# Dilated attention in a hybrid encoder layer: where the softmax's division stands

## The chip, the cores and the metric

The kernel runs on one core of a Trainium2 chip. The core has a matrix engine (PE, with its weight loads shown as PEld), a vector engine (DVE), a scalar engine (ACT), a general engine (POOL), a queue engine that issues most transfers (SP) and 16 DMA engines. The metric is the device time of one execution, in microseconds. Each engine runs its instructions in order; they wait for each other by semaphores.

## The reference

One layer of an encoder over 512 tokens of width 2048, all in float32: a retention branch and a dilated attention branch side by side, gated and merged, then a layer of 16,384 single-neuron experts of which each token takes 16 for each of 8 heads. The change is in the attention branch alone. Cut to that:

```python
ATT_SEGMENTS = ((128, 1), (512, 4), (2048, 16))      # (window, dilation), 8 heads of 128 each
s = einsum('nbihd,nbjhd->nbhij', qb, kb) * d ** -0.5 # masked outside the window
m = max(s, -1); p = exp(s - m); l = sum(p, -1)
o = einsum('nbhij,nbjhd->nbihd', p / l, vb);  lse = m + log(l)
...
w = softmax(stack(lses), axis=0)                     # over the three (window, dilation) groups
o = einsum('gbsh,gbshd->bshd', w, stack(outs))
```

Since the groups are merged by their denominators, a head's three groups are one softmax: one maximum, one sum over the three groups' exponentials, and one weighted sum of their values. The kernel computes it so.

## The kernel before, in words

The 512 tokens are four tiles of 128 (tile r holds the tokens r, r+4, ...). The front of the kernel, `mixers(part, with_kv)`, runs twice: part 0 for one token tile (T = 1), with the keys and values of all tiles, and part 1 for the other three (T = 3). In each part two blocks `hb` of four attention heads follow the projections that they need, so there are four stretches of four heads: two of part 0, two of part 1. Weights come in chunks of 512 KB (`wraw`), which ACT splits into a high half (`whi`, L130) and DVE into a low half (`wlo`, L131); each chunk feeds matmuls `gB` (L146 to L148), three per tile and 128 rows.

One head (`att_head`, L412 to L482) goes so. PE makes scores into PSUM banks (`sc`, L429 for group 0, 128x512, L437 for groups 1 and 2, 128x128 per tile). DVE adds the mask, takes the maximum and writes them to `P0` and `P1` (L431, L439), and makes the negative maximum `nb`. ACT takes the exponentials in place and sums each row (L449, nine in part 1, three in part 0). DVE adds the three sums to `lt` and inverts it (L452 to L454). Then DVE multiplies the exponentials by `lt` (L461, L468), PE transposes them to `pT` (L462, L471), ACT copies these to SBUF (`pT1s` L464, `pT0s` L473), PE multiplies them with the values (L476, L478) and sums over keys into the bank `oT`, 128 columns per token tile. As written before, the values are the stationary operand and the result comes out with the head's dimensions on the partitions and the tokens along the row. ACT copies it to `aT` (L480), and SP stores it to DRAM (`attD`, L482), where the merge (L553) reads it later. All banks named here come from `psB`, a pool of four.

In part 1 the experts of part 0 are worked in between: POOL gathers rows of the expert tables (L753, 1 MB each) and DVE multiplies and sums them (`gr`, L762). `tick(inv, 2)` behind the reciprocal places two such products behind it in DVE's order, and weight chunks place more by `tick(low, 0.85)`.

Which instruction follows which on an engine isn't the order of the code. A scheduler sets it when the kernel is built, from dependencies, free buffers and its own estimates; weight matmuls of the next projection are put between the instructions of the heads.

Of the kernel before, what the change touches and what calls it, by code (L numbers as in the profile page):

```python
# [10 lines left out]
F32 = mybir.dt.float32  # L11
# [4 lines left out]
AF = mybir.ActivationFunctionType  # L16
ALU = mybir.AluOpType
AX = mybir.AxisListType

P = 128  # L20
# [7 lines left out]
HD = 128  # L28
# [36 lines left out]
def hybrid_layer(ctx, tc, I, out, dbg=None):  # L65
    nc = tc.nc
# [33 lines left out]
    ident = const.tile([P, P], F32, name="ident")  # L100
# [3 lines left out]
    def bank(name, pool=None):  # L104
        return (pool or psB).tile([P, 512], F32, name=name, tag="bank")
# [49 lines left out]
    with tc.tile_pool(name="x0", bufs=1) as x0:  # L155
# [22 lines left out]
        for k in range(KT):  # L178
            ps = bank("xT")
# [28 lines left out]
    def mixers(part, with_kv):  # L208

        t0, T = (0, 1) if part == 0 else (1, NT - 1)  # L210
        mine = h_all[t0:t0 + T]
        N = T * P
        KV = 4 if with_kv else 5
        ctx2 = ExitStack()
        wk = ctx2.enter_context(tc.tile_pool(name=f"wk{part}", bufs=1, reuse_waits="tile"))
# [196 lines left out]
        def att_head(hb, h, qTs, scs):  # L412
            ks, vs = [], []
# [9 lines left out]
            p0 = wk.tile([P, T, 512], F32, name="P0", tag="P0", bufs=2)  # L423
            p1 = [wk.tile([P, T, P], F32, name="P1", tag="P1", bufs=4) for _ in range(2)]
            mx = wk.tile([P, 3, T], F32, name="mx", tag="mx", bufs=2)
            ls = wk.tile([P, 3, T], F32, name="ls", tag="ls", bufs=2)
            for t in range(T):
                ps = bank("sc")
# [4 lines left out]
            for g in (1, 2):  # L433
                ps = bank("sc")
                for t in range(T):
                    o = ps[:, t * P:(t + 1) * P]
                    nc.tensor.matmul(o, qTs[g][:, h, t * P:(t + 1) * P], ks[g][:, t * P:(t + 1) * P],  # L437
                                     start=True, stop=True)
# [12 lines left out]
            lt = wk.tile([P, T], F32, name="lt", tag="lt", bufs=2)  # L451
# [5 lines left out]
            pTs = []  # L457
            for g in (1, 2):
                ps = bank("pT1")
                for t in range(T):  # L460
                    nc.vector.tensor_scalar(p1[g - 1][:, t], p1[g - 1][:, t], lt[:, t:t + 1], None, op0=ALU.mult)  # L461
                    nc.tensor.transpose(ps[:, t * P:(t + 1) * P], p1[g - 1][:, t], ident)  # L462
                pT = wk.tile([P, N], F32, name="pT1s", tag="row", bufs=4)
                nc.scalar.copy(pT, ps[:, :N])  # L464
                pTs.append(pT)
            oT = bank("oT")
            for t in range(T):
                nc.vector.tensor_scalar(p0[:, t], p0[:, t], lt[:, t:t + 1], None, op0=ALU.mult)  # L468
                ps = bank("pT0")
                for s in range(NT):  # L470
                    nc.tensor.transpose(ps[:, s * P:(s + 1) * P], p0[:, t, s * P:(s + 1) * P], ident)  # L471
                pT = wk.tile([P, 512], F32, name="pT0s", tag="pT0s", bufs=2)
                nc.scalar.copy(pT, ps)  # L473
                o = oT[:, t * P:(t + 1) * P]
                for s in range(NT):
                    nc.tensor.matmul(o, vs[0][:, s], pT[:, s * P:(s + 1) * P], start=s == 0, stop=False)  # L476
                for g in (1, 2):
                    nc.tensor.matmul(o, vs[g][:, t], pTs[g - 1][:, t * P:(t + 1) * P], start=False, stop=g == 2)  # L478
            r = wk.tile([P, N], F32, name="aT", tag="row", bufs=4)
            nc.scalar.copy(r, oT[:, :N])  # L480
            k = hb * 4 + h
            nc.sync.dma_start(attD[part][k * P:(k + 1) * P], r)  # L482

# [27 lines left out]
        for n, c in [("gr", 0), ("gr", 1)] if with_kv else [("ga", 2), ("ga", 3)]:  # L511
            ps = gemm((w_in, COLS[n] + c * 512, h_all[1:]))[0]
# [276 lines left out]
    with tc.tile_pool(name="mgA", bufs=1, reuse_waits="tile") as mg, \  # L789
# [3 lines left out]
        h2, row, tiles2 = merge(0, mg, [(mg, 0, 1)])  # L793
# [78 lines left out]
    with tc.tile_pool(name="mgO", bufs=1, reuse_waits="tile") as mgO:  # L872
        with tc.tile_pool(name="mgB", bufs=1, reuse_waits="tile") as mg:
            h2, row, tiles2 = merge(1, mg, [(mgO, 0, 1), (hc, 1, 2)])
# [3 lines left out]
        with tc.tile_pool(name="rtB", bufs=2, reuse_waits="tile") as rt:  # L878
# [3 lines left out]
            for i, src in enumerate((e1, e2, gates)):  # L882
                ps = bank("hkT")
# [8 lines left out]
    with tc.tile_pool(name="gb", bufs=1, reuse_waits="tile") as gb:  # L892
# [6 lines left out]
        for blk in range(NB):  # L899
# [3 lines left out]
            for o in range(TB // OB):  # L903
# [7 lines left out]
                for q in range(OB // 4):  # L911
                    ps = bank("gg")
# [124 lines left out]
```

## Time and profile before

| | |
|---|---|
| time, median of 3 runs | 4641.93 us (4641.48 to 4642.64) |
| the profiled execution | 4638.18 us, of which span 4636.4 us |
| PE busy | 4230.3 us, 91% |
| DVE busy | 3462.9 us, 75% |
| ACT busy | 1913.0 us, 41% |
| POOL busy | 792.9 us, 17% |
| DMA, mean | 293 GB/s, 1358.77 MB |
| mean granted clock of PE | 0.959 of full |

A row of a view by time begins with its start from the beginning of the span and its duration; the bracket at its end is the time that the engine stood idle before it and the instruction that ended it. `out<-in` are the program's names of tiles; `x6` means six alike in a row. A view of waits gives, for an engine, its instruction, whom it waited for, the total, how many times, and the longest.

### The profile page before, as it was taken

How to read it: one execution, taken by the hardware profiler on the slowest of the kernel's cores; microseconds unless marked ns; L12 is line 12 of the kernel's file. 1: busy time of each engine (PE TensorE's matmuls, PEld its weight loads, DVE VectorE, ACT ScalarE, POOL GpSimd, SP SyncE). 2: the span in 40 equal slices, each digit the busy share in tenths (PEclk: the TensorE clock that was granted, in tenths of full speed). 3: DMA queues.
4: the chain of work that ended last, by engine and by line, in shares of the span. 5: the costliest groups of instructions: out<-in, count | busy, mean ns of one | idle time of the engine just before them, and what ended most of it. 6: DMA issues, size and time to landing. Idle time of an engine off the chain costs nothing.

```text
span 4636.4 us, 57934 instructions
## 1 busy us (share of the span) xinstructions
PE 4230.3 (91%) x21606; PEld 3542.0 (76%) x21606; DVE 3462.9 (75%) x4591; ACT 1913.0 (41%) x2642; POOL 792.9 (17%) x516
## 2 busy tenths in 40 slices
PE   8999998988998999889879987886799999999999
PEld 6888777765776878767667866686679998899997
DVE  7454555546666878577678968888678998999997
ACT  6444555545542333333332333344434343444433
POOL 0000000000001112122222221012112332334432
PEclk9999998999999999989889998998899999999999
DMA  7766675768658888778689895267889999999997
GB/s 247 225 219 224 213 240 177 245 200 279 214 192 305 329 310 329 271 278 323 249 328 375 336 357 193 92 219 295 311 304 348 402 400 398 395 404 402 404 400 294
DMA packets 510170, 1358.77 MB, mean 293 GB/s; under 512 B 49216, under 2 KB 129088, under 8 KB 440768
## 3 DMA queue, kind: packets, MB, share of 16 engines
q1 hardware_dynamic: 432800, 816.00, 50.6%
q0 software_dynamic: 73728, 536.90, 29.5%
q8 instruction: 169, 2.77, 0.2%
q10 hardware_dynamic: 3360, 2.17, 0.2%
q14 instruction: 113, 0.93, 0.1%
HBM read 1290.05 MB, written 64.88 MB: 292 GB/s over the span
## 4 chain that ended last, share of the span: by engine, by line
PE 44%; issue 20%; DMA 16%; DVE 12%; POOL 4%; ACT 4%; SPq 0%; POOLq 0%; ACTq 0%; DVEq 0%
PE gB L147 10%; PE gB L148 10%; PE gB L146 9%; POOL gr L753 4%; DMA wraw<-in_w_in 4%; DVE wlo L131 2%; DMA wraw<-in_w_out 2%; PE psa L853 2%; PE psa L851 2%; PE psa L852 2%; PE psy L978 2%; ACT whi L130 2%; PE psy L979 2%; PE psy L977 2%; DVE accg L771 2%
## 5 line engine op out<-in xcount | busy, mean ns | idle before, releaser
L131 DVE TENSOR_TENSOR wlo<-wraw,whi 128x1024 fp32r<-128x1024 f32 x752 | 916.4, 1222 | 650.6 <-ACT whi L130 633.5
L130 ACT CAST whi<-wraw 128x1024 fp32r<-128x1024 f32 x752 | 788.6, 1051 | 1190.4 <-PE gB L148 872.5
L753 POOL DMA_INDIRECT gr<-in_peer_u,eid x256 | 356.6, 1393 | 2776.8 <-DVE eid L740 1532.2
L771 DVE SCALAR_TENSOR_TENSOR accg<-gr,wg,accg 128x2048 f32<-128x2048 f32 x256 | 600.2, 2345 | 44.8 <-DMA gr<-in_peer_v,eid 31.4
L851 PE MATMUL psa<-rh,uh 128*128 128x256 f32 x2048 | 581.1, 284 | 32.7 <-ACT uh L836 32.7
L762 DVE SCALAR_TENSOR_TENSOR gr<-gr,hrow 128x2048 f32<-128x2048 f32 x256 | 583.7, 2283 | 35.7 <-DMA gr<-in_peer_u,eid 33.5
L753 POOL DMA_INDIRECT gr<-in_peer_v,eid x256 | 436.1, 1704 | 1009.0 <-DVE accg L771 849.4
L853 PE MATMUL psa<-rh,ul 128*128 128x256 f32 x2048 | 580.6, 284 | 9.4 <-DVE ul L837 9.4
L852 PE MATMUL psa<-rl,uh 128*128 128x256 f32 x2048 | 578.9, 283 | 0.0
L836 ACT CAST uh<-ur 128x1024 fp32r<-128x1024 f32 x256 | 269.0, 1052 | 474.2 <-DMA ur<-in_u_feat 307.0
L978 PE MATMUL psy<-vl,wh 128*128 128x512 f32 x1024 | 405.9, 396 | 17.6 <-DVE vl L971 17.4
L851 PEld LDWEIGHTS psa<-rh,uh 128*128 128x128 f32 x2048 | 390.3, 191 | 38.0 <-ACT uh L836 33.7
L977 PE MATMUL psy<-vh,wh 128*128 128x512 f32 x1024 | 403.5, 394 | 7.5 <-ACT vh L970 7.5
L979 PE MATMUL psy<-vh,wl 128*128 128x512 f32 x1024 | 401.6, 392 | 0.0
L852 PEld LDWEIGHTS psa<-rl,uh 128*128 128x128 f32 x2048 | 396.9, 194 | 4.1
L853 PEld LDWEIGHTS psa<-rh,ul 128*128 128x128 f32 x2048 | 389.7, 190 | 11.8 <-DVE ul L837 11.6
L970 ACT CAST vh<-vr 128x1024 fp32r<-128x1024 f32 x256 | 268.0, 1050 | 298.9 <-PE psy L979 157.7
L971 DVE TENSOR_TENSOR vl<-vr,vh 128x1024 fp32r<-128x1024 f32 x256 | 310.0, 1219 | 75.6 <-ACT vh L970 74.2
L147 PE MATMUL gB<-wlo,rh 128*128 128x512 f32 x768 | 315.8, 411 | 49.9 <-DVE wlo L131 49.1
L837 DVE TENSOR_TENSOR ul<-ur,uh 128x1024 fp32r<-128x1024 f32 x256 | 310.9, 1218 | 59.3 <-ACT uh L836 59.2
L146 PE MATMUL gB<-whi,rh 128*128 128x512 f32 x768 | 308.8, 405 | 29.7 <-ACT rh L567 20.8
L148 PE MATMUL gB<-whi,rl 128*128 128x512 f32 x768 | 310.8, 405 | 0.8 <-DVE rl L568 0.7
(466 smaller groups left out, 7978.6 us busy)
## 6 DMA issues: line engine op xcount, KB each, us to landing
wraw<-in_w_in SPq DMA_DIRECT2D x528, 512.0 KB
ur<-in_u_feat SPq DMA_DIRECT2D x256, 512.0 KB
vr<-in_peer_v SPq DMA_DIRECT2D x256, 512.0 KB
wraw<-in_w_ret_out SPq DMA_DIRECT2D x64, 512.0 KB
wraw<-in_w_out SPq DMA_DIRECT2D x64, 512.0 KB
wraw<-in_peer_w_query SPq DMA_DIRECT2D x64, 512.0 KB
wraw<-in_w_attn_out SPq DMA_DIRECT2D x32, 512.0 KB
GD<-Gs SPq DMA_DIRECT2D x4, 4096.0 KB
```

The source lines that it names most:

```text
L130: nc.scalar.copy(whi, raw)
L131: low = nc.vector.tensor_sub(wlo, raw, whi.bitcast(F32))
L146: nc.tensor.matmul(ps[t], ah(k), whi[:, j], start=first, stop=False)
L147: nc.tensor.matmul(ps[t], ah(k), wlo[:, j], start=False, stop=False)
L148: nc.tensor.matmul(ps[t], al(k), whi[:, j], start=False, stop=last)
L753: nc.gpsimd.indirect_dma_start(out=r, out_offset=None, in_=pu if s < P else pv_, in_offset=bass.IndirectOffsetOnAxis(ap=u.eid[:, s % P:s % ...
L762: nc.vector.scalar_tensor_tensor(r, r, 1.0, u.hrow, op0=ALU.mult, op1=ALU.mult, accum_out=u.ag[:, s:s + 1])
L771: nc.vector.scalar_tensor_tensor(u.acc, r, u.wg[:, s - P:s - P + 1], u.acc, op0=ALU.mult, op1=ALU.add)
L851: nc.tensor.matmul(psa[:, j], uh[:, cs], chi[k], start=k == 0, stop=False)
L852: nc.tensor.matmul(psa[:, j], uh[:, cs], clo[k], start=False, stop=False)
L853: nc.tensor.matmul(psa[:, j], ul[:, cs], chi[k], start=False, stop=k == KT - 1)
L978: nc.tensor.matmul(ps[:, t], wh[:, j, ts_], vl[:, j], start=False, stop=False)
```

## The change

The exponentials are no longer multiplied by 1/sum before their transposes. The products take the transposed exponentials as the stationary operand and the values as the moving one, so that a token tile's result has the tokens on the partitions; ACT multiplies it by `lt` as it empties PSUM into a new tile `o8`, PE transposes `o8` into a bank `aT`, and ACT copies that to the tile that is stored, whose layout is as before.

```diff
--- before.py
+++ after.py
@@ -458,14 +458,13 @@
             for g in (1, 2):
                 ps = bank("pT1")
                 for t in range(T):
-                    nc.vector.tensor_scalar(p1[g - 1][:, t], p1[g - 1][:, t], lt[:, t:t + 1], None, op0=ALU.mult)
                     nc.tensor.transpose(ps[:, t * P:(t + 1) * P], p1[g - 1][:, t], ident)
                 pT = wk.tile([P, N], F32, name="pT1s", tag="row", bufs=4)
                 nc.scalar.copy(pT, ps[:, :N])
                 pTs.append(pT)
+            o8 = wk.tile([P, T, HD], F32, name="o8", tag="row", bufs=4)
             oT = bank("oT")
             for t in range(T):
-                nc.vector.tensor_scalar(p0[:, t], p0[:, t], lt[:, t:t + 1], None, op0=ALU.mult)
                 ps = bank("pT0")
                 for s in range(NT):
                     nc.tensor.transpose(ps[:, s * P:(s + 1) * P], p0[:, t, s * P:(s + 1) * P], ident)
@@ -473,11 +472,15 @@
                 nc.scalar.copy(pT, ps)
                 o = oT[:, t * P:(t + 1) * P]
                 for s in range(NT):
-                    nc.tensor.matmul(o, vs[0][:, s], pT[:, s * P:(s + 1) * P], start=s == 0, stop=False)
+                    nc.tensor.matmul(o, pT[:, s * P:(s + 1) * P], vs[0][:, s], start=s == 0, stop=False)
                 for g in (1, 2):
-                    nc.tensor.matmul(o, vs[g][:, t], pTs[g - 1][:, t * P:(t + 1) * P], start=False, stop=g == 2)
+                    nc.tensor.matmul(o, pTs[g - 1][:, t * P:(t + 1) * P], vs[g][:, t], start=False, stop=g == 2)
+                nc.scalar.activation(o8[:, t], o, AF.Copy, scale=lt[:, t:t + 1])
+            ps = bank("aT")
+            for t in range(T):
+                nc.tensor.transpose(ps[:, t * P:(t + 1) * P], o8[:, t], ident)
             r = wk.tile([P, N], F32, name="aT", tag="row", bufs=4)
-            nc.scalar.copy(r, oT[:, :N])
+            nc.scalar.copy(r, ps[:, :N])
             k = hb * 4 + h
             nc.sync.dma_start(attD[part][k * P:(k + 1) * P], r)
```

Per head that is 3T fewer instructions on DVE, T more on ACT and T more on PE; over both parts 96 fewer, 32 more and 32 more. In the new code L461 are the transposes of groups 1 and 2, L470 those of group 0, L475 and L477 the products, L478 the eviction, L481 the transposes of `o8`, L483 the copy, L762 is L765. How the order moves, at three places:

PE, first head of the first stretch of part 1, before, from the last weight matmuls to the first tile's products; the numbers in names tell buffers apart, `pT1` and `pT0` are banks, `DVE_49`, `Activation_49` and `DMAHW4_49` semaphores of DVE, ACT and a DMA queue:

```order
L146 MATMUL gB_14803<-whi_14861,hR4h_191 128x512
L146 MATMUL gB_14804<-whi_14861,hR4h_191 128x512
L462 MATMUL pT1_14351<-ident_72,P1_14299 128x128 [waits DVE_49] x3
L462 MATMUL pT1_14360<-ident_72,P1_14300 128x128 [waits DVE_49] x3
L471 MATMUL pT0_14371<-ident_72,P0_14298 128x128 [waits DVE_49]
L471 MATMUL pT0_14371<-ident_72,P0_14298 128x128 x3
L476 MATMUL oT_14369<-pT0s_14376,avh_14292 128x128 [waits Activation_49]
L476 MATMUL oT_14369<-pT0s_14376,avh_14292 128x128 x3
L478 MATMUL oT_14369<-pT1s_14358,avh_14294 128x128 [waits DMAHW4_49]
L478 MATMUL oT_14369<-pT1s_14367,avh_14296 128x128 [waits DMAHW7_49]
```

and the same place of the change:

```order
L461 MATMUL pT1_14359<-ident_72,P1_14307 128x128 [waits Activation_49]
L147 MATMUL gB_14808<-wlo_14839,hR3h_178 128x512
L148 MATMUL gB_14808<-whi_14838,hR3l_179 128x512
L461 MATMUL pT1_14359<-ident_72,P1_14307 128x128 [waits Activation_49]
L461 MATMUL pT1_14365<-ident_72,P1_14308 128x128 [waits Activation_49]
L470 MATMUL pT0_14373<-ident_72,P0_14306 128x128 [waits DVE_49]
L470 MATMUL pT0_14373<-ident_72,P0_14306 128x128 x3
L461 MATMUL pT1_14365<-ident_72,P1_14308 128x128 [waits Activation_49] x2
L475 MATMUL oT_14372<-avh_14300,pT0s_14378 128x128 [waits DVE_49,Activation_49]
L475 MATMUL oT_14372<-avh_14300,pT0s_14378 128x128 x3
L477 MATMUL oT_14372<-avh_14302,pT1s_14363 128x128 [waits DMAHW4_49]
L477 MATMUL oT_14372<-avh_14304,pT1s_14369 128x128 [waits DMAHW7_49]
```

The first transposes waited for DVE and wait for ACT's exponentials now, and stand among the weight matmuls; the products have their operands exchanged, and behind the weight matmuls nothing of DVE's multiplies is waited for.

PE a little later in the same head, before, from the transposes of the third tile to the next head's score matmuls (`sc`); the three `pT0s` are the three token tiles:

```order
L471 MATMUL pT0_14399<-ident_72,P0_14298 128x128 [waits DVE_49,PE_49]
L471 MATMUL pT0_14399<-ident_72,P0_14298 128x128 x3
L429 MATMUL sc_14432<-akh_14415,aqT_12796 128x512 [waits DMAHW2_49,PE_49]
L476 MATMUL oT_14369<-pT0s_14390,avh_14292 128x128 [waits Activation_49]
L476 MATMUL oT_14369<-pT0s_14390,avh_14292 128x128 x3
L478 MATMUL oT_14369<-pT1s_14358,avh_14294 128x128
L478 MATMUL oT_14369<-pT1s_14367,avh_14296 128x128
L476 MATMUL oT_14369<-pT0s_14404,avh_14292 128x128 [waits Activation_49]
L476 MATMUL oT_14369<-pT0s_14404,avh_14292 128x128 x3
L478 MATMUL oT_14369<-pT1s_14358,avh_14294 128x128
L478 MATMUL oT_14369<-pT1s_14367,avh_14296 128x128
L429 MATMUL sc_14435<-akh_14415,aqT_12796 128x512 [waits PE_49]
```

and in the change, where the first tile's ScalarE eviction `o8` is waited for by `aT`:

```order
L146 MATMUL gB_14806<-whi_14865,hR4h_191 128x512
L475 MATMUL oT_14372<-avh_14300,pT0s_14392 128x128 [waits Activation_49]
L475 MATMUL oT_14372<-avh_14300,pT0s_14392 128x128 x3
L477 MATMUL oT_14372<-avh_14302,pT1s_14363 128x128
L477 MATMUL oT_14372<-avh_14304,pT1s_14369 128x128
L429 MATMUL sc_14439<-akh_14422,aqT_12804 128x512 [waits DMAHW2_49,PE_49]
L475 MATMUL oT_14372<-avh_14300,pT0s_14406 128x128 [waits Activation_49]
L475 MATMUL oT_14372<-avh_14300,pT0s_14406 128x128 x3
L477 MATMUL oT_14372<-avh_14302,pT1s_14363 128x128
L477 MATMUL oT_14372<-avh_14304,pT1s_14369 128x128
L481 MATMUL aT_14415<-ident_72,o8_14371 128x128
L429 MATMUL sc_14442<-akh_14422,aqT_12804 128x512 [waits PE_49]
```

The transposes of `o8` (the first stands one row ahead of these) and a score matmul now lie between the products of the three tiles. On ACT the two whi, which stood behind the exponentials and ahead of `pT1s`, now stand behind the first `pT0s` and ahead of the first `o8`.

DVE at the last head of that stretch, before, from behind the multiplies to the weight half that the next projection starts with (`gr` are expert products, `rs0`, `rt` and `tm3` belong to the projection's norm and rotation):

```order
L762 SCALAR_TENSOR_TENSOR gr_14736,ag_10632<-gr_14736,hrow_10630 128x2048 [waits DMASW7_49]
L762 SCALAR_TENSOR_TENSOR gr_14812,ag_10632<-gr_14812,hrow_10630 128x2048 [waits DMASW0_49,DVE_49]
L762 SCALAR_TENSOR_TENSOR gr_14839,ag_10632<-gr_14839,hrow_10630 128x2048 [waits DMASW1_49,DVE_49]
L400 TENSOR_REDUCE rs0_15024<-sq3_15022 128x12 [waits Activation_49]
L762 SCALAR_TENSOR_TENSOR gr_14890,ag_10632<-gr_14890,hrow_10630 128x2048 [waits DMASW2_49,DVE_49]
L402 RECIPROCAL rs0_15024<-rs0_15024 128x12 [waits Activation_49]
L762 SCALAR_TENSOR_TENSOR gr_14917,ag_10632<-gr_14917,hrow_10630 128x2048 [waits DMASW3_49,DVE_49]
L404 TENSOR_SCALAR rs0_15024<-rs0_15024 128x12 [waits DVE_49]
L256 TENSOR_TENSOR rt0_15029<-tm3_15018,rgt_12545 128x192
L257 TENSOR_TENSOR rt1_15030<-tm3_15018,rgt_12545 128x192
L258 TENSOR_TENSOR rt2_15031<-tm3_15018,rgt_12545 128x192
L131 TENSOR_TENSOR wlo_15065<-wraw_15062,whi_15064 128x1024 [waits DMAHW4_49,PE_49]
```

and in the change, from behind the reciprocal:

```order
L765 SCALAR_TENSOR_TENSOR gr_14485,ag_10640<-gr_14485,hrow_10638 128x2048 [waits DMASW3_49]
L765 SCALAR_TENSOR_TENSOR gr_14610,ag_10640<-gr_14610,hrow_10638 128x2048 [waits DMASW4_49]
L765 SCALAR_TENSOR_TENSOR gr_14741,ag_10640<-gr_14741,hrow_10638 128x2048 [waits DMASW7_49]
L400 TENSOR_REDUCE rs0_15028<-sq3_15026 128x12 [waits Activation_49]
L765 SCALAR_TENSOR_TENSOR gr_14816,ag_10640<-gr_14816,hrow_10638 128x2048 [waits DMASW0_49,DVE_49]
L402 RECIPROCAL rs0_15028<-rs0_15028 128x12 [waits Activation_49]
L765 SCALAR_TENSOR_TENSOR gr_14843,ag_10640<-gr_14843,hrow_10638 128x2048 [waits DMASW1_49,DVE_49]
L404 TENSOR_SCALAR rs0_15028<-rs0_15028 128x12 [waits DVE_49]
L256 TENSOR_TENSOR rt0_15033<-tm3_15022,rgt_12553 128x192
L257 TENSOR_TENSOR rt1_15034<-tm3_15022,rgt_12553 128x192
L258 TENSOR_TENSOR rt2_15035<-tm3_15022,rgt_12553 128x192
L131 TENSOR_TENSOR wlo_15096<-wraw_15093,whi_15095 128x1024 [waits DMAHW4_49,PE_49]
```

Two gathers of the row ahead are gone from before the weight half, as are the multiplies, and the chunk before it (`wlo_15069`) has moved ahead of the reciprocal.

## Rows read from the trace of the kernel before

**Rows 1.** Window, length, busy us (instructions) of PE, PEld, DVE, ACT, POOL; clock; DMA; GB/s

```profile
903.00:940.00 37.00, 35.88 (x191) 28.52 (x191) 20.47 (x66) 20.83 (x49) 0.00 (x0) 1.00 0.64 212
1905.00:2020.00 115.00, 91.46 (x438) 72.65 (x436) 68.50 (x175) 49.05 (x113) 20.00 (x13) 0.82 0.62 213
...
2241.00:2357.00 116.00, 97.57 (x458) 76.45 (x457) 65.14 (x161) 47.98 (x113) 21.02 (x12) 0.82 0.55 194
2357.00:2400.00 43.00, 28.90 (x125) 22.93 (x123) 31.89 (x18) 9.21 (x11) 14.96 (x11) 0.90 0.99 379
```

**Rows 2.** PE's waits, first stretch of part 1: total us, times, longest us

```profile
PE pT L462 <- DVE P L461: 10.6, 4, 3.1
PE gB L147 <- DVE wlo L131: 9.9, 1, 9.9
PE gB L146 <- ACT whi L130: 5.4, 4, 2.4
PE oT L476 <- ACT pT0s L473: 2.8, 4, 0.7
```

**Rows 3.** PE's waits, second stretch of part 1

```profile
PE pT L462 <- DVE P L461: 12.1, 7, 2.9
PE gB L146 <- ACT whi L130: 3.5, 4, 1.0
```

**Rows 4.** DVE in order of time, one head: start, duration, instruction, count, idle before

```profile
1917.99 2.26 DVE L762 SCALAR_TENSOR_TENSOR gr<-gr,hrow 128x2048 f32<-128x2048 f32 x1
...
1922.39 1.26 DVE L461 TENSOR_SCALAR P<-P,lt 128x128 f32<-128x128 f32 x6
1923.56 1.27 DVE L468 TENSOR_SCALAR P<-P,lt 128x512 f32<-128x512 f32 x3
```

**Rows 5.** PE in order of time, the same head and the next one's start

```profile
1922.72 1.56 PE L462 MATMUL pT<-ident,P 128*128 128x128 f32 x6 [3.10 <-DVE P L461]
...
1925.89 2.08 PE L476 MATMUL oT<-pT0s,avh 128*128 128x128 f32 x8 [0.68 <-ACT pT0s L473]
1927.76 1.06 PE L478 MATMUL oT<-pT1s,avh 128*128 128x128 f32 x4
1928.61 1.92 PE L471 MATMUL pT<-ident,P 128*128 128x128 f32 x8
...
1931.33 1.05 PE L476 MATMUL oT<-pT0s,avh 128*128 128x128 f32 x8
1932.22 0.61 PE L478 MATMUL oT<-pT1s,avh 128*128 128x128 f32 x4
...
1949.96 1.55 PE L462 MATMUL pT<-ident,P 128*128 128x128 f32 x6 [3.11 <-DVE P L461]
```

**Rows 6.** ACT in order of time, the same head

```profile
1917.57 1.98 ACT L130 CAST whi<-wraw 128x1024 fp32r<-128x1024 f32 x2
...
1925.25 0.59 ACT L473 COPY pT0s<-pT 128x512 f32<-128x512 f32 x1 [0.45 <-PE pT L471]
```

**Rows 7.** PE between weight matmuls and scores of the next head

```profile
1936.41 0.39 PE L148 MATMUL gB<-whi,hR4l 128*128 128x512 f32 x1
1936.64 0.40 PE L146 MATMUL gB<-whi,hR5h 128*128 128x512 f32 x1
1936.90 0.49 PE L437 MATMUL sc<-akh,aqT 128*128 128x128 f32 x2
...
1937.45 0.38 PE L437 MATMUL sc<-akh,aqT 128*128 128x128 f32 x2
```

**Rows 8.** DVE and PE at the end of the first stretch of part 1

```profile
2014.34 2.29 DVE L762 SCALAR_TENSOR_TENSOR gr<-gr,hrow 128x2048 f32<-128x2048 f32 x1 [2.17 <-DMA gr<-in_peer_u,eid]
...
2023.97 1.21 DVE L131 TENSOR_TENSOR wlo<-wraw,whi 128x1024 fp32r<-128x1024 f32 x1
...
2025.23 0.80 PE L147 MATMUL gB<-wlo,hR0h 128*128 128x512 f32 x1 [9.94 <-DVE wlo L131]
```

**Rows 9.** PE's waits, first stretch of part 0

```profile
PE pT L462 <- DVE P L461: 8.0, 2, 4.0
```

## Prediction

> **What bounds the kernel now.** I read the page's first table, then the stretches in which the attention heads run, then PE's waits in them, then one head on PE and on DVE. PE is busy for nine tenths of the span, by the table above: time is won only where PE stands still or runs at the lower clock. The change touches four stretches of four heads each: 665 to 709 and 903 to 940 us (part 0, one token tile per head) and 1905 to 2020 and 2241 to 2357 us (part 1, three token tiles per head). In both stretches of part 1 PE is busy 91.46 of 115 and 97.57 of 116 us at a mean granted clock of 0.82, so some of the busy time is at the lower of its two levels (1.2 against 2.4 GHz); no other engine reaches 70 us there and DMA is at 0.62 and 0.55. In 903 to 940 PE is busy 35.88 of 37 us at clock 1.00 [rows 1]. So part 1 has something to give, the second stretch of part 0 has not.
>
> What PE waits for in part 1: the scaled exponentials (L461), 10.6 us in the first stretch and 12.1 in the second, then weight halves and transposed tiles out of ACT [rows 2, 3]. One head shows why. When the exponentials are done and their sum is inverted, DVE takes the product for an expert gather first (L762, 2.26 us from 1917.99, and a second one behind it) and comes to L461 at 1922.39 [rows 4]. PE stands 3.10 us, starts its transposes at 1922.72, and the first eight product passes take 2.08 us where a later eight take 1.05, since the idle time before them left the clock at the lower level [rows 5]. From one head's first transposes to the next head's are 1949.96 - 1922.72 = 27.24 us [rows 5].
>
> **The change part by part.** *The multiplies go.* In a part 1 head these are six L461 (1.26 us) and three L468 (1.27 us) [rows 4]. DVE is no bound, so their time counts only by what stood behind them: the transposes now wait for ACT's exponentials alone, and PE can take them between weight matmuls while ACT is still at the last exponentials (the new order has them there). The wait on L461 goes: 10.6 + 12.1 = 22.7 us over eight heads [rows 2, 3], 2.84 each. With the transposes early, ACT's weight split (whi) stands behind the pT copies and no longer has PE idle on both sides; the waits on whi of 5.4 + 3.5 us [rows 2, 3] are 1.1 a head. The lower clock costs 2.08 - 1.05 = 1.03 us on L476 and 1.06 - 0.61 = 0.45 on L478 [rows 5]: 1.48 a head. The wait for the first pT0s, 2.8 us in four heads [rows 2], is 0.7 a head; it can't go wholly, since after the last exponential ACT still has copies like that of 0.59 us [rows 6] to make, so I let 0.3 of it stay. To be had: 2.84 + 1.1 + 1.48 + 0.7 = 6.12 us a head.
>
> *The product by token* has as many matmuls as before with the operands exchanged, all 128x128: the same 0.13 us a pass (1.05 / 8), costed at nothing. What it could cost is that the stationary side now comes late from ACT and can't be loaded ahead: one load per tile, under 0.3 us, inside the 0.3 above.
>
> *The added transposes* are on PE: 32, of which 24 in part 1. Eight transposes took 1.92 us [rows 5], 0.24 each: 0.72 a head.
>
> *Queues and buffers.* POOL's order is the same. SP still issues one store of aT a head, with loads for later heads behind it, and since aT comes earlier in time it holds nothing longer. A head now takes four tiles of the tag row from four buffers instead of three: each takes the buffer of its namesake of the head before, read 22 us earlier, so nothing waits for it.
>
> *The added evictions* are on ACT, 32 of 128x128. The trace has no such one with a scale; a PSUM copy four times as wide took 0.59 us [rows 6], so it lies between nothing and 0.6; with ACT busy 49.05 of 115 us [rows 1] I take 0.3 and let it hide. But there are two new waits of PE. First, all token tiles share the bank oT, and the next tile's products wait until ACT has emptied the one before. The nearest rows are the scores of three tiles in one bank, which DVE empties in turn: the steps stand at 1936.90 and 1937.45, 0.55 apart, with one weight matmul between [rows 7]. Two such steps a head, 16 in part 1, are 8.8 us if nothing lay between; in the new order eight transposes or a score matmul or weight matmuls lie in each, so I charge 0.1 a head.
>
> The Trainium skill, in "PSUM — Partial Sum Buffer", section "PSUM bank collisions raise a hardware error", says that two engines must not be in one bank at once and that one has to guard by bank, not by address, which speaks against three tiles in one bank with an eviction after each; the steps in the rows agree with it. By that rule with nothing between, the sum would be about 8 us less; the rows of the new order are why I don't take it.
>
> Second, a transpose of o8 waits for its eviction, and o8 of the first tile stands behind two whi on ACT (1.98 us together [rows 6]). PE has eight transposes (1.92 us) to do in that time, so the first is covered; the last tile's has a score matmul on either side of it.
>
> So a part 1 head saves 6.12 - 0.72 - 0.1 - 0.3 = 5.0 us: 27.2 becomes about 22.2.
>
> *The end of the first stretch of part 1.* There PE waits 9.94 us for a weight's low half (wlo), which DVE makes at 2023.97 behind seven gathers, each fed by its DMA (one of them waited 2.17 us for it) [rows 8]. In the new order the first chunk's wlo stands ahead of the head's reciprocal and five gathers instead of seven stand before the second. A chunk has 18 weight matmuls 0.23 us apart [rows 7], 4.1 us that PE can do earlier, and two gathers of some 2.3 us leave the way: 4.6. That is 8.7 us at most, which also must pay for that head's own 5.0; I take 8 for this head in all. If the gathers' DMA sets the pace it is nearer to 0.
>
> *The end of the second.* From 2357 us DMA is at 0.99 and PE busy 28.90 of 43 us [rows 1]: what follows is set by DMA. Work that comes there sooner may just wait. I take half of the last head: 2.5.
>
> *Part 0.* No gather stands between sum and multiply here; the wait of 8.0 us on L461 [rows 9] is a wait for the exponentials and stays as a wait for ACT. A head saves two or three small multiplies on the chain (about 0.6) and gets an eviction, a transpose and their hand-overs (about 0.85); eight heads, four of them in a stretch where PE is full and each transpose counts: +2 us, between -2 and +6.
>
> Sum: first stretch 3 x 5.0 + 8 = 23, second 3 x 5.0 + 2.5 = 17.5, part 0 +2: -38.5 us. The profiled execution took 4638.18 us, 3.75 below the median of the timed runs, 4641.93; against itself it becomes 4599.7, against the median 4603.4. Everything after the stretches just moves forward: merge and experts start from the same data, earlier.
>
> **The rivals.** *Half of it comes back as waits on ACT.* PE runs in order, the transposes of o8 wait for evictions, the evictions for whi; if each head pays the 1.98 us of whi and a second 0.3, a head saves 2.7: 8 x 2.7 + 4 at the first end - 2 = 24 us less, 4618. For it: the order has o8 behind whi. Against it: there are matmuls enough between. 0.23.
>
> *DMA and the gathers set the pace.* The gathers are 1 MB each and follow the program; after both stretches DMA is at 0.9 and more. If the second stretch's gain and the end of the first are taken back there, 15 - 2 = 13 us stay: 4629. For it: 0.99 after 2357 us, the gather that waited 2.17 us. Against it: DMA is at 0.62 and 0.55 in the stretches, and what DMA has to bring starts earlier as well. 0.12.
>
> *Slower: the head's end becomes a chain.* Every token tile goes product, eviction, transpose, and the next head's scores stand behind the transposes in PE's order. If nothing lies between, each of the 32 pays a hand-over like that for pT0s (2.8 / 4 = 0.7 us [rows 2]) and its transpose 0.24: 30 us, and what the L461 wait gave is then only the multiplies' own 1.26 x 8 = 10 us, because PE would wait for the exponentials instead of the gathers: +20, about 4660. It decides where the scores of the next head come later than before in a head's course. For it: part 0, where nothing else is at hand. Against it: in part 1 the order spreads scores and weight matmuls between. 0.07.
>
> *More than I say:* all of 6.12 - 0.72 in eight heads, the 9.94 us gone beside it, part 0 at -2: 55 us less, 4587; a part of my forecast's range.
>
> **How the numbers follow.** The forecast (4603, its own range 4587 to 4612) has 0.54, the rivals 0.23, 0.12 and 0.07; 0.04 is left for no change, where the neighbours eat it all. What a measurement of this kernel tells from no change is 0.2%, 9 us, so faster is below 4632.6. The forecast and the first rival lie there; of the second's 0.12, which stands close to the bound, 0.07 is faster, 0.04 no change and 0.01 slower: faster 0.84, same 0.08, slower 0.08. The range goes from 4584 to 4631: the upper end takes in the first two rivals.
>
> **What would show it.** In the changed profile PE should have no wait on a DVE multiply; the clock in the two part 1 stretches should be near 1.00; a head should take 22 us from transposes to transposes; the stretches should shrink by about 20 us and 15 us, and the 9.94 us wait to a few. The first rival shows as PE waits of aT on o8 or oT on ACT of over 1 us a head, the second as full heads' gains with longer waits on wlo or whi behind the stretches, the third as a period over 27 us. I am wrong if the L461 wait comes back under another name (the exponentials) at the same size.

## The result, and the profile after

The changed kernel took 4596.07 us (median of four runs, 4584.69 to 4604.74) against 4642.28 for the kernel before: a ratio of 0.9885, 95% interval 0.9869 to 0.9901. A second set of runs beside the experiments gave 4595.85 us and 0.9901 (0.9883 to 0.9919). The forecast was 4603 us, or a ratio of 0.9917. The profiled execution took 4602.08 us, its span is 4600.3.

Busy time in the two stretches of part 1, after, with the columns of [rows 1]:

```profile
1905.00:2020.00 115.00, 100.22 (x532) 79.55 (x532) 76.52 (x161) 58.32 (x132) 27.04 (x17) 0.96 0.75 268
2241.00:2357.00 116.00, 104.18 (x554) 83.03 (x552) 74.55 (x115) 55.50 (x128) 28.34 (x19) 0.99 0.73 262
```

The granted clock is 0.96 and 0.99 where it was 0.82 [rows 1] (0.96 and 0.95 in the second profiled execution). The windows hold 532 and 554 matmuls instead of 438 and 458, but the program isn't at the same point in them; what was gained is read from the marks below. PE's waits in the first of them, after, which answer to [rows 2]:

```profile
PE gB L147 <- DVE wlo L131: 8.3, 2, 7.5
PE sc L437 <- DVE mx L439: 2.8, 1, 2.8
PE oT L475 <- ACT pT0s L472: 2.1, 2, 1.1
PE gB L146 <- ACT whi L130: 1.6, 1, 1.6
```

and all those in the second ([rows 3]):

```profile
PE gB L147 <- DVE wlo L131: 5.3, 3, 3.1
PE oT L475 <- ACT pT0s L472: 1.1, 1, 1.1
PE gB L146 <- ACT whi L130: 0.8, 1, 0.8
```

The waits on L461, 10.6 and 12.1 us, are gone, and no wait on the exponentials has taken their place in part 1. None for the new `o8` is there either. Waits on wlo have grown: between the marks shown below they are 13.1 us instead of 12.7 in the first stretch and 12.7 instead of 9.0 in the second. One head on PE, after (compare [rows 5]; weight matmuls between them left out):

```profile
1931.84 0.27 PE L461 MATMUL pT<-ident,P 128*128 128x128 f32 x1
...
1934.50 1.16 PE L475 MATMUL oT<-avh,pT0s 128*128 128x128 f32 x8 [1.06 <-ACT pT0s L472]
1935.50 0.61 PE L477 MATMUL oT<-avh,pT1s 128*128 128x128 f32 x4
1935.95 1.04 PE L470 MATMUL pT<-ident,P 128*128 128x128 f32 x8
1936.82 0.27 PE L481 MATMUL aT<-ident,o 128*128 128x128 f32 x1
```

The first products take 1.16 us where they took 2.08, eight transposes 1.04 where they took 1.92, and the transpose of `o8` (`o` in the trace) starts without an idle bracket. ACT in the same head:

```profile
1931.84 0.48 ACT L449 ACTIVATE P<-P,nb,rs 128x128 f32<-128x128 f32 x1
...
1933.86 0.59 ACT L472 COPY pT0s<-pT 128x512 f32<-128x512 f32 x1
1934.34 2.00 ACT L130 CAST whi<-wraw 128x1024 fp32r<-128x1024 f32 x2
1936.23 0.38 ACT L478 ACTIVATE o<-oT,lt 128x128 f32<-128x128 f32 x1
```

The first transposes ran while the last exponential (1931.84) was only beginning. The scaled eviction is 0.38 us long and starts right behind the two whi, at 1936.23; PE needs it at 1936.82.

To see where the time came from, four instructions that both kernels have serve as marks: the squares (L398) ahead of the first stretch of part 1 and behind it, those ahead of the second stretch, and the first cast of the experts' query (L567, after L570). Before:

```profile
1836.15 1.48 ACT L398 ACTIVATE sq<-tm 128x1536 f32<-128x1536 f32 x1
2063.27 1.48 ACT L398 ACTIVATE sq<-tm 128x1536 f32<-128x1536 f32 x1
2174.95 1.49 ACT L398 ACTIVATE sq<-tm 128x1536 f32<-128x1536 f32 x1
2616.98 1.04 ACT L567 CAST rh<-mT 128x128 fp32r<-128x128 f32 x5
```

After:

```profile
1848.51 1.48 ACT L398 ACTIVATE sq<-tm 128x1536 f32<-128x1536 f32 x1
2052.79 1.50 ACT L398 ACTIVATE sq<-tm 128x1536 f32<-128x1536 f32 x1
2164.01 1.49 ACT L398 ACTIVATE sq<-tm 128x1536 f32<-128x1536 f32 x1
2585.60 1.03 ACT L570 CAST rh<-mT 128x128 fp32r<-128x128 f32 x5
```

Across the first stretch: 204.28 instead of 227.12 us, 22.8 less. Across the second, with the merge: 421.59 instead of 442.03, 20.4 less. The second profiled execution of the changed kernel has 204.12 and 421.51. Two kernels with the same part 1 and another part 0 (the change in one part only, below) lie up to 3.2 us from their likes in these intervals.

PE in the two intervals, with the columns of [rows 1], before:

```profile
1836.15:2063.27 227.12, 194.37 (x885) 155.94 (x884) 153.25 (x263) 83.65 (x155) 46.85 (x35) 0.89 0.77 276
2174.95:2616.98 442.03, 395.58 (x1745) 318.86 (x1744) 336.58 (x389) 143.31 (x246) 104.36 (x77) 0.93 0.86 325
```

After:

```profile
1848.51:2052.79 204.28, 182.81 (x899) 145.67 (x898) 142.88 (x227) 85.99 (x167) 54.09 (x36) 0.97 0.83 304
2164.01:2585.60 421.59, 385.36 (x1757) 310.17 (x1756) 327.83 (x353) 146.12 (x258) 97.14 (x77) 0.96 0.91 341
```

So the gain has two halves of the same size. PE stands idle 11.3 and 10.2 us less, and it is busy 11.6 and 10.2 us less, with a few matmuls more but at a clock of 0.97 and 0.96 instead of 0.89 and 0.93.

Ahead of the first mark this execution was 12.4 us behind. In the fourteen profiled executions of this document the first mark stands between 1832.6 and 1848.5 us, and in the four whose program is that of the kernel before up to there, between 1833.5 and 1845.4. From the last mark to the end of the span are 2014.7 instead of 2019.4 us, where thirteen of the fourteen lie between 2008.1 and 2025.6. So neither difference can be told from what executions differ by.

### The profile page after: what moved, and what is told of

It is laid out like the page before. It is cut to its first block, busy times and chain, and to the rows that moved or that the text cites. A ratio compares the mean times of both kernels' runs of the same rounds, so it can differ in the third digit from the quotient of the medians.

```text
span 4600.3 us, 57918 instructions
## 1 busy us (share of the span) xinstructions
PE 4211.8 (92%) x21638; PEld 3524.4 (77%) x21638; DVE 3439.3 (75%) x4495; ACT 1917.0 (42%) x2674; POOL 795.5 (17%) x516
## 4 chain that ended last, share of the span: by engine, by line
PE 50%; DMA 18%; DVE 13%; issue 13%; ACT 3%; POOL 2%; SPq 0%; ACTq 0%; DVEq 0%; POOLq 0%
PE gB L147 9%; PE gB L148 9%; PE gB L146 9%; PE psy L981 3%; PE psy L982 3%; PE psy L980 3%; PE psa L856 3%; PE psa L854 3%; PE psa L855 3%; DMA gr<-in_peer_v,eid 3%; DMA ur<-in_u_feat 3%; DMA wraw<-in_w_in 2%; POOL gr L756 2%; DVE wlo L131 2%; DMA vr<-in_peer_v 2%
## 5 line engine op out<-in xcount | busy, mean ns | idle before, releaser
L765 DVE SCALAR_TENSOR_TENSOR gr<-gr,hrow 128x2048 f32<-128x2048 f32 x256 | 583.8, 2284 | 45.7 <-DMA gr<-in_peer_u,eid 44.2
```

Source lines behind the costliest of these rows:

```text
L765: nc.vector.scalar_tensor_tensor(r, r, 1.0, u.hrow, op0=ALU.mult, op1=ALU.mult, accum_out=u.ag[:, s:s + 1])
```

## The experiments

All are compared with the kernel before on the same chip; its medians there were 4642 to 4648 us. Theory A: the gain comes from the transposes no longer standing behind expert gathers in DVE's order. Theory B: it comes from the 96 multiplies that DVE is spared. Each edit brings a new order of instructions with it, so an experiment tests the two together. What is said of marks and intervals is read from one profiled execution each, and a difference of some 3 us in an interval is no finding.

**The change again.** 

> The changed kernel once more, beside the experiments. It took 4584.7 to 4604.7 us in four runs. Expected: 4590 to 4600 in the median, 42 to 52 us under the kernel before, with single runs up to 10 us away from it. If the four runs were a lucky sample and the predicted 38.5 us are the truth, 4603.

4595.85 us, ratio 0.9901 (0.9883 to 0.9919): the better of the two readings holds. Across the marks it saved 23 and 21 us.

**Multiplies kept, gathers behind them** (kernel before).

```diff
-            if not with_kv:
-                tick(inv, 2)
...
-                nc.vector.tensor_scalar(p0[:, t], p0[:, t], lt[:, t:t + 1], None, op0=ALU.mult)
+                inv = nc.vector.tensor_scalar(p0[:, t], p0[:, t], lt[:, t:t + 1], None, op0=ALU.mult)
...
+            if not with_kv:
+                tick(inv, 2)
             r = wk.tile([P, N], F32, name="aT", tag="row", bufs=4)
```

> The kernel before with all its multiplies; only the two expert products of each part 1 head are placed behind the head's last multiply instead of behind the reciprocal. Theory A (the gain of the change is that the transposes no longer stand behind the gathers on DVE): PE's wait on the multiplies falls from 2.8 to under 1 us a head, the clock in the two stretches of part 1 rises above 0.9, and 20 to 35 us of the change's gain come without it: 4607 to 4622. Theory B (it is the 96 multiplies taken off DVE that count): DVE has all its work still, so within 9 us of the kernel before, 4633 to 4651. What is missing from the change's time then is the price of the multiplies on the way, about 1.3 us a head, less the transposes that it adds.

4604.73 us, ratio 0.9924 (0.9905 to 0.9942). DVE has every multiply still, and most of the gain is there (35 of 46 us by the ratios, 2 us more than Theory A expected at best): Theory A holds and B falls. By the marks the second stretch has nearly all of it, 422.4 us against the change's 421.6, and the first 13.7 of 22.8 us; the wait on wlo there is 4.4 us longer than in the change, and the rest was not taken apart. DVE in one of its heads:

```profile
1925.15 0.18 DVE L454 RECIPROCAL lt<-lt 128x3 f32<-128x3 f32 x1
1925.36 1.27 DVE L459 TENSOR_SCALAR P<-P,lt 128x128 f32<-128x128 f32 x6
1926.55 1.27 DVE L466 TENSOR_SCALAR P<-P,lt 128x512 f32<-128x512 f32 x3
1927.73 2.28 DVE L762 SCALAR_TENSOR_TENSOR gr<-gr,hrow 128x2048 f32<-128x2048 f32 x1
```

and PE's first transposes there, with the wait that is left of 3.10 us:

```profile
1925.70 0.53 PE L460 MATMUL pT<-ident,P 128*128 128x128 f32 x2 [0.84 <-DVE P L459]
```

**No division at all**: the kernel before without L461 and L468.

> The kernel before without the multiplies and with nothing in their place: the division by the sum is left out, so the attention's output is undivided. It bounds what the change can give, and its distance from the change is the price of the evictions, transposes and hand-overs that the change adds. Theory A: 4580 to 4592, 4 to 16 us below the change (32 transposes of 0.24 us are 7.7). If the added work is wholly hidden: the change's own time, 4590 to 4600. If exchanging the operands of the product gave a gain of its own: above the change, over 4600.

4588.40 us, ratio 0.9886 (0.9868 to 0.9904): 7.5 us below the changed kernel by the medians, within what Theory A expected, though the intervals overlap.

**The eviction on DVE** (changed kernel).

```diff
-                nc.scalar.activation(o8[:, t], o, AF.Copy, scale=lt[:, t:t + 1])
+                nc.vector.tensor_scalar(o8[:, t], o, lt[:, t:t + 1], None, op0=ALU.mult)
```

> The changed kernel with the eviction of the product, times 1/sum, on DVE instead of ACT: 32 small instructions, of which the first of each part 1 head stands behind the two expert products on DVE again. Theory A: the transposes of o8, and behind them in PE's order the products of the next token tile and the next head's scores, wait for DVE, 2 to 4 us a head, and half to all of the gain is lost: 4615 to 4640. Theory B: DVE has 64 instructions less than before instead of 96, so a third of the gain at most is lost: 4596 to 4611.

4596.44 us, ratio 0.9899 (0.9882 to 0.9916): not told apart from the change, and my expectation under Theory A was wrong. (The median is at the lower edge of what Theory B expected, but B had fallen with the late gathers.) DVE has the gathers ahead of the eviction, as expected:

```profile
1931.90 0.18 DVE L454 RECIPROCAL lt<-lt 128x3 f32<-128x3 f32 x1
1932.00 2.26 DVE L765 SCALAR_TENSOR_TENSOR gr<-gr,hrow 128x2048 f32<-128x2048 f32 x1
...
1936.40 0.35 DVE L478 TENSOR_SCALAR o<-oT,lt 128x128 f32<-128x128 f32 x1
```

but PE comes to the transpose only later and doesn't wait:

```profile
1938.30 0.27 PE L481 MATMUL aT<-ident,o 128*128 128x128 f32 x1
```

So it is in six of the eight heads of part 1. In the last head of each stretch PE does wait, 2.5 and 4.2 us. In the first stretch that is behind an expert product whose gather came late:

```profile
2007.77 2.29 DVE L765 SCALAR_TENSOR_TENSOR gr<-gr,hrow 128x2048 f32<-128x2048 f32 x1 [1.26 <-DMA gr<-in_peer_u,eid]
...
2010.39 0.33 PE L481 MATMUL aT<-ident,o 128*128 128x128 f32 x1 [2.50 <-DVE o L478]
```

The two intervals are 2.8 and 1.6 us longer than the change's. So the gathers do little harm there, where 2 to 4 us in every head were expected. What counts is where in a head PE needs DVE: for the first transposes at once, for the division at the end 6.4 us after the reciprocal.

**The change in part 1 alone**, and **in part 0 alone** (`if part == 1:` and `if part == 0:` around the new code, the old in the other branch).

> The change in part 1 alone; part 0 keeps the multiplies and the old product. By the prediction part 0 costs 2 us (between -2 and +6), so this takes 0 to 6 us less than the whole change: 4588 to 4598. If part 0 gave a share of the gain (eight of the sixteen heads are there), this would lose some of it: over 4605.

> The change in part 0 alone; part 1 keeps the multiplies. By the prediction within 2 us below and 6 us above the kernel before, which took 4641 to 4647 in the median. If removing multiplies gains wherever it happens: 10 to 20 us below it.

4596.60 us, ratio 0.9896 (0.9876 to 0.9915), and 4640.59 us, ratio 0.9994 (0.9979 to 1.0010). All of the gain is in part 1. In the first stretch of part 0 of the changed kernel the wait on the multiplies of [rows 9] stands as a wait on the exponentials, and a new one on the eviction has come:

```profile
PE pT L461 <- ACT P L449: 5.4, 2, 2.7
...
PE aT L481 <- ACT o L478: 1.2, 3, 0.5
```

**Nothing transposed back** (changed kernel; `o8` goes to the store as it is).

```diff
-            ps = bank("aT")
-            for t in range(T):
-                nc.tensor.transpose(ps[:, t * P:(t + 1) * P], o8[:, t], ident)
-            r = wk.tile([P, N], F32, name="aT", tag="row", bufs=4)
-            nc.scalar.copy(r, ps[:, :N])
+            r = o8.rearrange("p t d -> p (t d)")
```

> The changed kernel with o8 stored as it is: the 32 transposes back and the copy behind them are left out, so the attention's output is stored transposed within each tile. Prices what the change adds on PE. By the sum, 24 transposes of 0.24 us in part 1 and the chain at the head's end in part 0: 6 to 12 us below the change, 4584 to 4590, as far down as the kernel without a division. If transposes hide beside ACT's and DVE's work: the change's own 4590 to 4600.

4586.23 us, ratio 0.9882 (0.9862 to 0.9902): by the medians the transposes and their copy cost 9.6 us, inside 6 to 12, again with intervals that overlap. The two intervals between marks are 1.8 and 3.4 us shorter than the change's.

**A bank for each tile's product** (changed kernel; `oT = bank("oT")` moved into the loop over t).

> The changed kernel with a PSUM bank of its own for each token tile's product, so that a tile's products don't wait for ACT to empty the tile before. The prediction charged 0.1 us a head for the shared bank: 0 to 2 us below the change, 4590 to 4600. If the hand-overs through one bank cost what the score rows show, 0.5 us twice a head: 8 us below, 4582 to 4590. If the three banks out of a pool of four hold up the next head's scores: above 4600.

4602.93 us, ratio 0.9910 (0.9890 to 0.9930), not told apart from the change, though the median lies where the third reading has it. By the marks its two intervals are 8.4 and 5.9 us longer than the change's, with 7.5 us of waits on pT0s in 12 places against 3.2 in 3. So own banks seem to cost something themselves, and the run doesn't price the shared bank alone. That the shared bank costs little is seen in the change: in part 1 of neither of its two executions does the list of waits have products (L475) waiting for an eviction (L478).

**Clock and wait taken apart** (kernel before, part 1).

```diff
+            if part == 1:
+                dm = bank("dm")
+                for i in range(12):
+                    nc.tensor.matmul(dm[:T, :P], ls[:, 2], ident, start=True, stop=True)
             pTs = []
```

> The kernel before, with twelve small matmuls a part 1 head that nobody reads (row sums against the identity, 3 x 128, about 0.2 us each), put on PE where it waits for the multiplies. It parts the clock from the wait. The prediction gave the clock 1.48 us a head: if so, the first eight product passes take about 1.05 us instead of 2.08, the mean clock in both stretches of part 1 rises above 0.9, and the time falls by 8 to 12 us to 4630 to 4636 while the transposes still start when DVE lets them. If the lower clock costs nothing that counts, or the added matmuls delay weight matmuls by as much: 4640 to 4652.

4633.54 us, ratio 0.9982 (0.9967 to 0.9998): 8 us, just clear of noise, from matmuls that nobody needs. The clock in the two stretches is 0.94 and 0.97, and one head on PE reads:

```profile
1919.53 2.78 PE L460 MATMUL dm<-ident,ls 128*3 128x128 f32 x24
1924.54 1.30 PE L466 MATMUL pT<-ident,P 128*128 128x128 f32 x6 [1.33 <-DVE P L465]
...
1927.24 1.16 PE L480 MATMUL oT<-pT0s,avh 128*128 128x128 f32 x8 [0.67 <-ACT pT0s L477]
1928.24 0.61 PE L482 MATMUL oT<-pT1s,avh 128*128 128x128 f32 x4
1928.69 1.04 PE L475 MATMUL pT<-ident,P 128*128 128x128 f32 x8
```

The transposes start when DVE lets them, as before; from there on these rows run at the upper level. The added matmuls take 2.78 us a head; without them PE's busy time between the marks would be 187.9 and 386.7 us (an estimate: 198.99 and 397.79 less four times 2.78) instead of 194.37 and 395.58, 1.9 us a head less. That speaks for a share of the clock in the change's gain. But not all of it comes through here: the first interval is 3.1 us longer than before, with new waits of 4.6 us on the maxima and 2.9 us more on wlo, and the second 4.6 us shorter. Where the 8 us lie was not settled.

**The division inside the transposes** (kernel before; the diagonal stands in the moving operand).

```diff
+            dg = wk.tile([P, T, P], F32, name="dg", tag="row", bufs=4)
+            for t in range(T):
+                inv = nc.vector.tensor_scalar(dg[:, t], ident, lt[:, t:t + 1], None, op0=ALU.mult)
...
-                    nc.tensor.transpose(ps[:, s * P:(s + 1) * P], p0[:, t, s * P:(s + 1) * P], ident)
+                    nc.tensor.matmul(ps[:, s * P:(s + 1) * P], p0[:, t, s * P:(s + 1) * P], dg[:, t], start=True, stop=True)
```

> The division in a third place: the transposes of the undivided exponentials take a diagonal matrix of the inverse sums as their moving operand instead of the identity (three 128x128 multiplies on DVE a part 1 head make it, ahead of the gathers), so that they divide as they transpose; the product is as before and nothing is transposed back. Theory A: no gather ahead of what PE waits for, no added transposes, but the transposes wait for the sum, about 1 us a head more than in the change: between the kernel without a division and the one with late gathers, 4588 to 4604. If the overlap of the transposes with the exponentials is what counts: no better than late gathers, 4600 to 4612.

4620.23 us, ratio 0.9943 (0.9923 to 0.9963): worse than both theories had it. The wait on DVE is 0.93 us a head at most; but eight of these 128x128 matmuls

```profile
1932.89 1.95 PE L472 MATMUL pT<-dg,P 128*128 128x128 f32 x16
```

stand as 16 passes and take 1.95 us where eight transposes took 1.04 in eight passes. With 18 in a part 1 head that is 18 x 0.11 = 2.0 us, 16 us in eight heads, and some 5 us in part 0, where a head has six. PE's busy time between the marks is 6.4 and 5.5 us above that of the late gathers. But the intervals themselves are 0.8 us shorter and 6.0 longer than there; most of the 15.5 us that the medians lie apart isn't found in them. So the doubled passes are one cause, and how much of the loss is theirs stays open. Nor does the run say what the overlap with the exponentials is worth.

**The last head's gathers left for later** (changed kernel; `if not with_kv and h < 3: tick(inv, 2)`).

> The changed kernel without the two expert products that stand behind the reciprocal of the last head of each block of part 1; they follow later in the program instead. It tests the wait on wlo that is left at the end of the first stretch, 6 to 7.5 us, where the gathers are ahead of the weight half in DVE's order. If their number ahead of it sets that wait: 4 to 8 us below the change, 4584 to 4592. If the DMA of the gathers sets it, or the products come back ahead of some later weight half: no change, 4590 to 4600.

4604.81 us, ratio 0.9915 (0.9897 to 0.9933): no gain, and above both readings. Its two intervals are 2.2 and 7.1 us shorter than the change's. At the fourth mark it was 23.5 us ahead of the changed kernel's 2585.60, of which 13.2 lie ahead of the first mark, where executions differ:

```profile
2562.09 1.04 ACT L570 CAST rh<-mT 128x128 fp32r<-128x128 f32 x5
```

Window, length and busy time as in [rows 1], from the last mark to the end, first this kernel:

```profile
2562.00:4594.00 2032.00, 1840.86 (x11134) 1633.71 (x11132) 1759.28 (x2156) 793.52 (x1047) 542.94 (x301) 0.96 0.87 329
```

then the change:

```profile
2585.00:4600.00 2015.00, 1838.50 (x11139) 1632.37 (x11137) 1750.70 (x2153) 792.17 (x1047) 531.10 (x297) 0.96 0.87 330
```

PE's work is the same, but POOL has four gathers more to bring (301 against 297), and the rest is 17 us longer. PE waits 43.5 us for wlo in it, against 33.1 to 35.7 in six other executions (before, the change twice, part 1 only, own banks, earlier gathers). That gathers which are put off are paid for there fits this, but it rests on one execution, and another kernel's rest is 2025.6 us long without any put off.

**The same gathers, earlier.** As in the last, with `tick(inv, 2 if h == 2 else 3)`, so that eight are placed in the first three heads and the balance is kept.

> The changed kernel with the two expert products of each block's last head of part 1 spread over the three heads before it (three, three and two more by the credit instead of two each and two), so that as many are done by the end of the block as in the change, and none stands behind the last head's reciprocal. Without the last head's products alone the kernel had been ahead of the change by 15 to 20 us at 2617 us and lost it again by the end. If it was the lateness of four gathers that lost it: 8 to 15 us below the change, 4580 to 4590. If the gathers now ahead of the maxima hold up the next exponentials, or the experts' part gives the lead back whatever comes before: 4594 to 4610.

4582.34 us, ratio 0.9862 (0.9840 to 0.9883), some 14 us below the change by the medians and the fastest of the kernels that compute the whole. The two intervals are 198.0 and 416.3 us, 6.3 and 5.3 less than the change's. The fourth mark stands at 2566.52, 19 us ahead of the change, 9.3 of it already at the first mark,

```profile
2566.52 1.03 ACT L570 CAST rh<-mT 128x128 fp32r<-128x128 f32 x5
```

and the rest of its span of 4580.7 us, 2014.2, is as long as the change's 2014.7. Its interval overlaps the first of the change's (0.9869 to 0.9901) and only touches the second (0.9883 to 0.9919), and the two were not run side by side: probably faster, not proven. The wait at the end of the first stretch is 6.6 us still, so it was not only the number of gathers behind the reciprocal that mattered.

## Why the prediction was right, point by point

*The wait on the multiplies goes.* Right, and the reason too: late gathers alone, with all multiplies, give most of the gain, 35 of 46 us. What the rest of it is (the multiplies, the earlier transposes, the wlo at the first end) was not taken apart.

*The parts of the sum.* First stretch: 23 us forecast, 22.8 in the first profiled execution. Second: 17.5 forecast, 20.4; the 2.9 us between them are about the half head that I had given away to the full DMA behind it. Part 0: +2 forecast, -3 measured by the ratio of the run with part 0 alone, between -10 and +5 by its interval; its 0.6 and 0.85 us a head were not worked out from rows. What lies beyond, some 5 us between the last mark and the end, has no term in the sum and isn't told from what executions differ by.

*The clock* was the term that I mis-sized. I gave it 1.48 us a head, from the products alone. The transposes of before ran at the lower level as well: eight in 1.92 us [rows 5] against 1.04 after, 0.24 and 0.13 each. The rows of the 18 transposes of a head add up to 1.56 + 1.12 + 1.92 = 4.6 us, so about 2 us a head were missing; the three that the change adds cost 0.4 us instead of 0.72. The run with idle matmuls fits this with its 1.9 us a head of busy time, and with the 8 us (1 to 15) that it gained.

*What I counted too well* hides the same amount. The wait on wlo at the end of the first stretch is 7.5 us (6.2 in the second execution) where I had it at a few; there is one of 2.8 us of scores on DVE's reduction that I didn't have; the first pT0s still costs 1.1 us in some heads. Of the 5.0 us a head the sum had 0.76 from shorter busy time (1.48 for the clock less 0.72 for the transposes) and 4.24 from waits. Measured between the marks, both gave 2.7. That the total came so near is in part luck: the clock was priced too low and the waits too high by amounts that nearly cancel.

*The period of a head*, 22 us, holds in the mean only. From first transposes to the next head's it is 18.1, 19.2 and 26.1 us, 21.1 in the mean (27.3 before). The fourth head's first transposes start here, before and after:

```profile
2004.57 1.55 PE L462 MATMUL pT<-ident,P 128*128 128x128 f32 x6 [1.27 <-DVE P L461]
...
1994.90 0.27 PE L461 MATMUL pT<-ident,P 128*128 128x128 f32 x1
```

From the first mark to there 168.42 us have become 146.39, 22.0 less; from there to the next mark 58.70 have become 57.89, 0.8 less (2.1 in the second execution). So the 8 us for the last head with the stretch's end was mis-sized: the end gave next to nothing, and what the stretch gained lies ahead of that head's transposes, where the sum had less.

*The scaled eviction.* I wrote that the trace before has no such one of 128x128. It has: L248 scales 128x128 out of PSUM, 40 times, at 0.37 us in the mean, which is what the new ones take. The 0.3 that I took was near.

*The rivals.* Waits on ACT: none of `o8` on the way in part 1, whi lay as close ahead of it as feared, and its eviction ended at 1936.61, 0.2 us before PE came to it. Gathers and DMA as the pace: not for the change, which keeps their number and place, but the execution of the kernel that put four off looks like it, in the experts' part and not where I looked. The chain at the head's end exists in part 0 only, up to 1.0 us at a time and 2.7 us in all; that it cancels what the multiplies gave there is not shown, only that the change in part 0 alone gained nothing.

*The shared PSUM bank.* The charge of 0.1 us a head is borne out by the change, which has no wait for it in part 1; in the order, other matmuls lie in each hand-over. The kernel with earlier gathers has one, of 2.4 us. The rule that the prediction took from the Trainium skill ("PSUM — Partial Sum Buffer", "PSUM bank collisions raise a hardware error") speaks of what must not be at once; in the change's rows keeping to it had no price that its waits show.

## What to carry to other kernels

A division of softmax is best placed not where it is cheapest to compute but where the engine that makes it isn't waited for: the same DVE behind the same gathers cost 2.8 us a head ahead of the transposes and, behind the product, 6.7 us of waits in two of eight heads. Where PE runs at the lower clock behind a wait, price the whole group behind it, transposes too: here shorter busy time was half of the gain. Try first whether moving the other work (here one line) does most of what rewriting does. And where background transfers are placed by hand, watch their number up to each point: with four of them put off the last part was 17 us longer in one execution, and with the same number placed earlier the lead was kept.

## What the runs showed of the hardware

Eight float32 128x128 matmuls against a diagonal matrix took 16 passes and 1.95 us, eight transposes of the same size 8 passes and 1.04 us. Matmuls whose result nobody reads, twelve a head, raised the mean granted clock of both stretches from 0.82 to 0.94 and 0.97, with a time of 0.9982 (0.9967 to 0.9998) of the one before. A copy of 128x128 out of PSUM with a scale took ACT 0.37 us.
